# When the mixing stage's results are gated, and in which order the last rows leave

## The chip, the core and the metric

The kernel runs on one core of a Trainium2 chip. The metric is the device time of one execution in microseconds (us); the figure compared is the median of several runs. The engines are TensorE (PE, matmuls and transposes), VectorE (DVE), ScalarE (ACT), GpSimd (POOL) and SyncE (SP, which here only issues DMAs). Each engine works through its own queue in order.

## The reference

One decoder layer over 2048 rows of width 1024, in float32:

```python
u = x * (1 + scale) + shift                  # scale, shift, gate from SiLU(c) @ W_ada
q, k, v, a_gate, p_in, p_gate, m_a, m_p = split(u @ W_in)
a = (sliding_window_attention_with_sinks(q, k, v) * silu(a_gate)) @ W_attn_proj
p = (group_linear(causal_pool(p_in)) * pool_scale * silu(p_gate)) @ W_pool_proj
y = (sigmoid(m_a) * a + sigmoid(m_p) * p) @ W_out * (1 + gate)
x = layer_norm(alpha * x + y) * ln_gain + ln_bias
```

## The kernel before

Every large matrix product is done by blocks: a *quad* multiplies two row blocks of weights with a resident activation of two column halves, and gets its four 128 x 512 results by seven block products instead of eight (a Strassen-Winograd scheme, named B11, T1, T2, B21, T3, B22, T4 after the operand that the activation side holds). One operand set per name lies in SBUF (`sets`, shown by the profile as set_B or set_T). Float32 accuracy comes from splitting each operand into a rounded high part (cast on ACT) and a low part (a subtraction on DVE), and taking three of the four cross terms. So one product is 3 x 4 = 12 matmuls of 128 x 128 by 128 x 512.

Weights of a quad are split in pairs by `pair_split` (first, second and third pair), into four rotating tiles called w_set; T4's single block is split by `half_split`. High parts of these show up at lines 303 and 310, low parts at line 132 (`low`). Weights come by DMA as W and A; GpSimd prepares their sums (`sum1`, `mid`, `late`, lines 266 to 275).

Quads are worked on in groups of two. `back` finishes a group: for each quad T2 and B21, then T3 of the first quad, B22 of the first, T3 and B22 of the second, then both T4. `front` opens the next group: B11 and T1 of each of its quads. `ring` runs the groups of one phase. Each product is followed by `tick()`, which counts the steps (14 per group), runs the hooks written down for that position, and then whatever `defer(n, f)` put n ticks ahead. At the hooks stand the loads and splits of the next phase's operand sets (`set_steps`, with SPLIT_AT and FETCH_AT giving positions; those under 14 fall into the last group of a phase, the others into the first group of the next).

The results of a quad leave in the order B21's (first row block, first half), then after T3 (second block, second half, in the SBUF tile p5, summed at line 387), after B22 (first block, second half), and after T4 (second block, first half). `consume` takes each.

After attention come six phases in one block of code: a last gate group, then for each half s of the sequence an attention mix phase (`attn_quad`, two groups) and a pool mix phase (`pool_quad`, two groups), and an output phase (`out_quad`, four groups). In the mix phases `gates_ahead` loads the gates (ma or mp) from DRAM, half of them at the group's start and half two ticks later, and runs a sigmoid over each; `consume` multiplies each result by its gate (line 620, or 629), the pool quads also add it to the attention part (631) and store y.

In the output phase a result is added to alpha times x (line 709). Rows are normalised once both halves are there, rows 14 and 15 by `last_stats` and `last_norm` (680 to 696); the very last group is done one quad after the other by `finish_pairs`.

In the attention stages PE's work on scores and values is interleaved with quads that fill the gaps (`filling`). `take_p` sums the pool windows on GpSimd, then `second` scales and subtracts on DVE and multiplies on GpSimd. The attention loop starts each iteration on DVE with a reciprocal of the softmax sums; `closing` holds additions that are to follow it.

A scheduler sets the final order of each engine's queue: it goes by the order in which instructions were written down, and lets a later one go first where the earlier isn't ready by its own clock. Calls by `dve`, `act`, `pool`, `sp` are pinned behind the instruction that was written down just before them on that engine; calls by `nc.vector`, `nc.scalar` and so on are not.

Of the kernel before, what the change touches and what calls it, by code (L numbers as in the profile page):

```python
# [60 lines left out]
def kernel(  # L61
# [276 lines left out]
    def back(ph, grp, opened, nxt, own, tick):  # L338
# [5 lines left out]
        for q, (a, b, c, w, *copy) in zip(grp, opened):  # L344
# [19 lines left out]
            if len(copy) < 2:  # L364
                nc.vector.tensor_tensor(b, c, p5, ALU.add)
# [17 lines left out]
        def with_t3(x):  # L383
            q, b, c, p5 = st[x]
            product(c, w[x][1], "T3")
            tick()
            nc.vector.tensor_tensor(p5, c, p5, ALU.add)
# [20 lines left out]
        for q, b, c, p5 in st:  # L408
            product(c, lasts.pop(0) if lasts else half_split(ph, q.a22), "T4")
            tick()  # L410
            q.consume(ph, 1, 0, c)

    def finish_pairs(ph, grp, opened, tick):
# [18 lines left out]
        for x, q in enumerate(grp):  # L432
# [15 lines left out]
            tick()  # L448
            q.consume(ph, 0, 1, b)
            product(c, lasts[x], "T4")  # L450
# [56 lines left out]
    SPLIT_AT = (2, 3, 4, 5, 6, 7, 11, 12, 13, 14, 15, 16, 17, 18)  # L507
# [93 lines left out]
    def gates_ahead(name, s, m, raw):  # L601
        g = {}

        def ahead(ph, turn):
            for mi, t in (((0, 0), (1, 1)), ((0, 1), (1, 0)))[turn]:
                x = g[mi, t] = ph.c("g")
                sp.dma_start(x, gates_d[name][s, m + mi, t])
                if raw:
                    defer(1, lambda x=x: nc.scalar.activation(x, x, AF.Sigmoid))  # L609

        return g, ahead

    def attn_quad(s, m):
        g, ahead = gates_ahead("ma", s, m, True)

        def consume(ph, mi, t, src):
# [3 lines left out]
            nc.vector.tensor_tensor(ta[k][:, t * CH : (t + 1) * CH], src, g.pop((mi, t)), ALU.mult)  # L620

        return Quad((wap[m], wap[m + 1]), consume, ahead)

    def pool_quad(s, m):
        gates, ahead = gates_ahead("mp", s, m, True)

        def consume(ph, mi, t, src):
            g = gates.pop((mi, t))
            nc.vector.tensor_tensor(g, src, g, ALU.mult)
            dst = ta[m + mi][:, t * CH : (t + 1) * CH]  # L630
            nc.vector.tensor_tensor(dst, g, dst, ALU.add)
# [46 lines left out]

    def last_stats(row, n, zn):
        nc.vector.bn_stats(carry[:, row - 12, 6 * n : 6 * n + 6], zn)  # L680

    def last_norm(row, z):

        st, mv, rs = (carry[:, row - 12, a:b] for a, b in ((0, 12), (12, 14), (14, 15)))
        nc.vector.bn_aggr(mv, st)
        nc.vector.tensor_scalar(rs, mv[:, 1:2], EPS, None, ALU.add)
        nc.gpsimd.tensor_tensor(rs, rs, mhalf, ALU.pow)
        nc.vector.scalar_tensor_tensor(z, z, mv[:, 0:1], vec["gain"], ALU.subtract, ALU.mult)
        ending.append((row, z, rs))
        if row + 1 < S // P:  # L690
            return
        for row, z, rs in ending[::-1]:
            for n, q in enumerate((nc.sync, nc.scalar)):
                zn = cols(z, n)
                nc.vector.scalar_tensor_tensor(zn, zn, rs, cols(vec["lnb"], n), ALU.mult, ALU.add)
                q.dma_start(out[row * P : (row + 1) * P, n * CH : (n + 1) * CH], zn)

    ending = []
# [4 lines left out]
    def out_quad(k):  # L703
        def consume(ph, mi, n, src):
            row = k + mi
            z, n_done = zs[row]
            zs[row][1] += 1
            zn = cols(z, n)
            nc.vector.scalar_tensor_tensor(zn, zn, ALPHA, src, ALU.mult, ALU.add)
# [66 lines left out]
    def attention(ph, s, fills, post, opened):  # L776
# [56 lines left out]
        def take_p(m, t, acc):  # L833
# [841 lines left out]
```

## Time and profile before

| | us |
|---|---|
| median of 3 runs (1681.26 to 1681.58) | 1681.29 |
| the profiled execution | 1681.68 |
| its span, first to last instruction | 1679.9 |
| PE busy | 1642.9 |
| DVE busy | 1208.6 |
| ACT busy | 1026.3 |
| POOL busy | 949.3 |

A row of the timeline gives start, duration, engine, line of the code, operation, the tiles written and read, and in brackets how long the engine was idle before it and what ended that. Names are the tiles' names without numbers: mm, lg, pt and pv are accumulators in PSUM, w_set split weights, set_B and set_T operand sets, g a gate, wide a 128 x 1024 tile of rows, p the tile p5. A row with x12 joins that many instructions. A row of the busy time by stretch gives the stretch, its length, then busy time and count of PE, PEld (weight loads), DVE, ACT and POOL, the granted share of PE's clock, and the DMA share and rate.

### The profile page before, as it was taken

What the parts mean: (1) busy time and instruction counts of PE and PEld (TensorE: products, weight loads), DVE (VectorE), ACT (ScalarE), POOL (GpSimd) and SP (SyncE); (2) the same over time, 40 slices, a digit from 0 to 9 for tenths busy, and PEclk for the clock granted to TensorE, in tenths of its full rate; (3) what the DMA queues carried; (4) which work ended last, traced back from release to release, by engine and by line L of the source; (5) the groups of instructions that cost most, each with busy time, mean ns of one, the idle gap of its engine ahead of it and who ended that gap; (6) DMA issues with size and microseconds to landing.
All of it is one profiled execution on the core that took longest, in us unless ns stands there. A gap on an engine that the chain in (4) does not pass through costs nothing.

```text
span 1679.9 us, 24661 instructions
## 1 busy us (share of the span) xinstructions
PE 1642.9 (98%) x8058; PEld 1382.7 (82%) x8058; DVE 1208.6 (72%) x2156; ACT 1026.3 (61%) x2146; POOL 949.3 (57%) x710
## 2 busy tenths in 40 slices
PE   7999999999999999999999999999999999999997
PEld 6788888888888788888888888888878878878886
DVE  6955656676867867566467677777769896979777
ACT  4754547778778755334577777776647464554452
POOL 3343437585867838773376858597445453423442
PEclk9999999999999999999999999999999999999999
DMA  9688844343543578872432335345968896677443
GB/s 362 209 291 296 204 158 124 99 126 107 176 137 113 188 278 298 312 273 94 154 128 88 126 131 171 118 127 188 330 215 313 274 321 219 227 271 235 155 147 113
DMA packets 185971, 331.56 MB, mean 197 GB/s; under 512 B 18017, under 2 KB 43761, under 8 KB 185841
## 3 DMA queue, kind: packets, MB, share of 16 engines
q1 hardware_dynamic: 182720, 325.72, 56.8%
q10 hardware_dynamic: 3088, 4.23, 1.1%
q8 instruction: 64, 1.05, 0.3%
q14 instruction: 67, 0.54, 0.1%
q0 software_dynamic: 32, 0.02, 0.0%
HBM read 223.77 MB, written 109.28 MB: 198 GB/s over the span
## 4 chain that ended last, share of the span: by engine, by line
PE 80%; DVE 7%; DMA 5%; ACT 3%; issue 2%; POOL 2%; SPq 1%; POOLq 0%; DVEq 0%; ACTq 0%
PE mm L57 51%; PE lg L57 22%; PE pv L57 4%; PE pt L57 4%; DMA head_T<-in_wada_dram 1%; DMA g<-mp_d 1%; DVE w_set L132 1%; DVE L L57 1%; SPq L57 1%; DVE set_T L57 1%; DMA head_B<-in_wada_dram 1%; DVE room L57 1%; DVE w_set L57 0%; DMA g<-ma_d 0%; ACT g L609 0%
## 5 line engine op out<-in xcount | busy, mean ns | idle before, releaser
L57 PE MATMUL mm<-set_B,w_set 128*128 128x512 f32 x2664 | 652.6, 392 | 0.9 <-DVE w_set L57 0.4
L57 PEld LDWEIGHTS mm<-set_B,w_set 128*128 128x128 f32 x2664 | 495.8, 188 | 103.2 <-DVE w_set L57 0.8
L57 PE MATMUL mm<-set_T,w_set 128*128 128x512 f32 x1824 | 453.4, 395 | 2.1 <-DVE mm L57 1.2
L57 PE MATMUL lg<-set_T,w_set 128*128 128x512 f32 x1704 | 411.3, 391 | 7.6 <-ACT w_set L303 2.8
L57 PEld LDWEIGHTS mm<-set_T,w_set 128*128 128x128 f32 x1824 | 336.3, 188 | 70.8 <-DVE mm L57 4.2
L57 PEld LDWEIGHTS lg<-set_T,w_set 128*128 128x128 f32 x1704 | 319.6, 188 | 78.0 <-issue 3.7
L132 DVE TENSOR_TENSOR w_set<-W,w_set 128x1024 fp32r<-128x1024 f32 x137 | 192.5, 1405 | 142.3 <-ACT w_set L303 133.0
L303 ACT CAST w_set<-W 128x1024 fp32r<-128x1024 f32 x137 | 144.0, 1051 | 192.8 <-PE mm L57 148.3
L266 POOL TENSOR_TENSOR W<-W,A 128x512 f32<-128x512 f32 x46 | 73.5, 1598 | 271.6 <-DMA A<-in_win_dram 66.5
L57 POOL TENSOR_TENSOR w_set<-W,w_set 128x512 fp32r<-128x512 f32 x120 | 159.1, 1333 | 110.4 <-ACT w_set L57 108.6
L57 DVE TENSOR_TENSOR o<-pv,o 64x128 f32<-64x128 f32 x256 | 71.9, 281 | 96.8 <-ACT o L57 93.4
L57 POOL TENSOR_TENSOR W<-W 128x512 f32<-128x512 f32 x82 | 111.1, 1368 | 52.8 <-DVE sm L57 25.8
L57 ACT ACTIVATE L<-L,nm 128x257 f32<-128x257 f32 (+1 forms) x256 | 127.1, 498 | 17.8 <-DVE nm L57 8.2
L275 POOL TENSOR_TENSOR W<-W 128x512 f32<-128x512 f32 x46 | 71.9, 1563 | 103.9 <-DVE w_set L132 94.0
L270 POOL TENSOR_TENSOR W<-W 128x512 f32<-128x512 f32 x44 | 80.3, 1828 | 83.1 <-DVE w_set L132 66.7
L57 DVE CUSTOM_DVE_ANT_0 L<-lg,bt,nsink 128x256 f32<-128x256 f32 (+1 forms) x256 | 111.6, 473 | 15.2 <-DMA pg<-pg_d 10.8
L57 ACT CAST w_set<-W 128x512 fp32r<-128x512 f32 (+1 forms) x165 | 101.4, 628 | 24.4 <-POOL W L57 14.5
L57 ACT COPY o<-pv 64x256 f32<-64x256 f32 x128 | 47.3, 369 | 71.3 <-PE pv L57 70.1
L271 POOL TENSOR_TENSOR W<-W 128x512 f32<-128x512 f32 x44 | 69.1, 1570 | 32.4 <-DMA W<-in_win_dram 16.4
L57 ACT ACTIVATE L<-L,sm 128x256 f32<-128x256 f32 (+1 forms) x128 | 64.3, 502 | 36.6 <-DVE sm L57 36.2
L57 DVE TENSOR_TENSOR ptl<-pt,pth 128x512 fp32r<-128x512 f32 (+1 forms) x128 | 85.7, 669 | 1.0 <-ACT pth L57 0.9
L57 POOL TENSOR_TENSOR spare<-spare 128x512 f32<-128x512 f32 x48 | 80.2, 1679 | 8.1 <-ACT spare L57 6.0
(233 smaller groups left out, 2411.6 us busy)
## 6 DMA issues: line engine op xcount, KB each, us to landing
W<-in_win_dram SPq DMA_DIRECT2D x42, 512.0 KB, 5.8
W<-in_win_dram SPq DMA_DIRECT2D x42, 256.0 KB, 4.0
A<-in_win_dram SPq DMA_DIRECT2D x42, 256.0 KB, 4.9
ag_d<-sig SPq DMA_DIRECT2D x32, 256.0 KB, 5.9
pg_d<-sig SPq DMA_DIRECT2D x32, 256.0 KB, 4.4
pg<-pg_d SPq DMA_DIRECT2D x32, 256.0 KB, 3.2
pin_B<-fin SPq DMA_DIRECT2D x32, 256.0 KB, 2.0
ag<-ag_d SPq DMA_DIRECT2D x32, 256.0 KB, 3.1
```

The lines of the kernel that those rows point to most:

```text
L57: return lambda *args, **kw: self.tc.keep_in_program_order(op(*args, **kw))
L132: engine.tensor_tensor(dst, src, as32(hi), ALU.subtract)
L266: e.tensor_tensor(self.w[:, 1, :], self.w[:, 2, :], self.a22, ALU.add)
L270: e.tensor_tensor(x[:, 1, :], x[:, 1, :], x[:, 0, :], ALU.subtract)
L271: e.tensor_tensor(x[:, 2, :], x[:, 0, :], x[:, 2, :], ALU.subtract)
L275: e.tensor_tensor(x[:, 3, :], x[:, 3, :], x[:, 1, :], ALU.subtract)
L303: a.copy(by_two(hi), raw)
```

## The change

In the mix phases each result is gated two results later than before (`two_behind`): a result's use is kept until two more have come, the last two run one and two ticks after the group's last product. The multiplications and additions there are pinned (`dve`). The sigmoids are put off by 2, 3 or 4 ticks instead of 1. T4's blocks are split before the tick behind the first B22 instead of after it. The splits of set T2 move from positions 6 and 7 to 8 and 9. In the attention stages the pool scaling goes into `closing`, behind the next reciprocal. In the last quad B22 comes before T3, two results are added to their rows in two steps, T4 goes to an accumulator of its own, and the halves of row 14 leave before those of row 15, one of them before the last product's result.

```diff
@@ back
             if len(copy) < 2:
-                nc.vector.tensor_tensor(b, c, p5, ALU.add)
+                (dve if q.ahead else nc.vector).tensor_tensor(b, c, p5, ALU.add)
...
-            nc.vector.tensor_tensor(p5, c, p5, ALU.add)
+            (dve if q.ahead else nc.vector).tensor_tensor(p5, c, p5, ALU.add)
             q.consume(ph, 1, 1, p5)
-        def with_b22(x):
+        def with_b22(x, then=None):
             q, b, c, p5 = st[x]
             product(b, w[x][0], "B22")
+            if then:
+                then()
             tick()
...
             third(1)
-            with_b22(0)
-            lasts = [half_split(ph, q.a22) for q in grp]
+            with_b22(0, lambda: lasts.extend(half_split(ph, q.a22) for q in grp))
...
             q.consume(ph, 1, 0, c)
+        defer(1, lambda: use_up(1))
+        defer(2, use_up)
@@ finish_pairs, behind B21's consume
+            last = x + 1 == len(grp)
+            if last:
+                q.consume(ph, 1, 1, p5, True)
+                product(b, w3[0], "B22")
+                tick()
+                q.consume(ph, 0, 1, b)
             product(c, w3[1], "T3")
             tick()
-            nc.vector.tensor_tensor(p5, c, p5, ALU.add)
-            q.consume(ph, 1, 1, p5)
-            product(b, w3[0], "B22")
-            if x + 1 < len(grp):
+            if last:
+                q.consume(ph, 1, 1, c)
+                ending.pop(0)()
+                q.consume(ph, 1, 0, c, True)
+                c = a
+            else:
...
-            product(c, lasts[x], "T4")
+            product(c, lasts[x], "T4", last)
@@
-    SPLIT_AT = (2, 3, 4, 5, 6, 7, 11, 12, 13, 14, 15, 16, 17, 18)
+    SPLIT_AT = (2, 3, 4, 5, 8, 9, 11, 12, 13, 14, 15, 16, 17, 18)
@@ gates_ahead
-                    defer(1, lambda x=x: nc.scalar.activation(x, x, AF.Sigmoid))
+                    wait = {(0, 0): 2, (1, 1): 3, (0, 1): 2, (1, 0): 4}[mi, t]
+                    defer(wait, lambda x=x: nc.scalar.activation(x, x, AF.Sigmoid))
+    unused = []
+    def use_up(left=0):
+        while len(unused) > left:
+            unused.pop(0)()
+    def two_behind(use):
+        def consume(ph, mi, t, src):
+            use_up(1)
+            unused.append(lambda: use(ph, mi, t, src))
+        return consume
@@ attn_quad, pool_quad
-            nc.vector.tensor_tensor(ta[k][:, t * CH : (t + 1) * CH], src, g.pop((mi, t)), ALU.mult)
+            dve.tensor_tensor(ta[k][:, t * CH : (t + 1) * CH], src, g.pop((mi, t)), ALU.mult)
-        return Quad((wap[m], wap[m + 1]), consume, ahead)
+        return Quad((wap[m], wap[m + 1]), two_behind(consume), ahead)
-            nc.vector.tensor_tensor(g, src, g, ALU.mult)
+            dve.tensor_tensor(g, src, g, ALU.mult)
...
-            nc.vector.tensor_tensor(dst, g, dst, ALU.add)
-            defer(3, lambda: sp.dma_start(y_d[s, m + mi, t], dst))
-        return Quad((wpp[m], wpp[m + 1]), consume, ahead)
+            dve.tensor_tensor(dst, g, dst, ALU.add)
+            defer(1, lambda: sp.dma_start(y_d[s, m + mi, t], dst))
+        return Quad((wpp[m], wpp[m + 1]), two_behind(consume), ahead)
@@ rows 14 and 15
+    def last_halves(row, z, rs):
+        def half(n, q):
+            zn = cols(z, n)
+            dve.scalar_tensor_tensor(zn, zn, rs, cols(vec["lnb"], n), ALU.mult, ALU.add)
+            q.dma_start(out[row * P : (row + 1) * P, n * CH : (n + 1) * CH], zn)
+        return [lambda n=n, q=q: half(n, q) for n, q in enumerate((nc.sync, nc.scalar))]
...
-        ending.append((row, z, rs))
-        if row + 1 < S // P:
-            return
-        for row, z, rs in ending[::-1]:
-            for n, q in enumerate((nc.sync, nc.scalar)):
...
+        ending.extend(last_halves(row, z, rs))
+        if row + 1 == S // P:
+            for f in ending:
+                f()
@@ out_quad
+            e = dve if row > 13 else nc.vector
+            if (row, n) in begun:
+                e.tensor_tensor(zn, src, zn, ALU.add)
+            else:
+                e.scalar_tensor_tensor(zn, zn, ALPHA, src, ALU.mult, ALU.add)
+            if partly:
+                begun.add((row, n))
+                return
             zs[row][1] += 1
-            nc.vector.scalar_tensor_tensor(zn, zn, ALPHA, src, ALU.mult, ALU.add)
@@ take_p
             def second():
                 pg, p, copied = x
-                dve.scalar_tensor_tensor(
-                    p, p, 1.0 / POOL_W[m // 2], copied if own else acc, ALU.mult, ALU.subtract
-                )
-                pool.tensor_tensor(p, p, pg, ALU.mult)
+                def scaled():
+                    dve.scalar_tensor_tensor(
+                        p, p, 1.0 / POOL_W[m // 2], copied if own else acc, ALU.mult, ALU.subtract
+                    )
+                    pool.tensor_tensor(p, p, pg, ALU.mult)
+                closing.append(scaled)
                 later(n + wait + 1, lambda: keep_raw(pin_d[s], m, t, p))
@@ close, filling
             while closing:
-                x, name = closing.pop()
-                _, b, c, p5 = st[x]
-                dve.tensor_tensor(b if name == "T2" else p5, c, p5, ALU.add)
+                closing.pop(0)()
+        def add_up(x, name):
+            _, b, c, p5 = st[x]
+            dve.tensor_tensor(b if name == "T2" else p5, c, p5, ALU.add)
...
-                        closing.append((x, name))
+                        closing.insert(0, lambda x=x, name=name: add_up(x, name))
@@ behind the attention loop
         for _ in fill:
             pass
+        close()
         run_coming(True)
```

More of the change, by code (lines that the diff above doesn't have):

```diff
@@ L440, in finish_pairs @@
             q.consume(ph, 0, 0, a)
+            last = x + 1 == len(grp)
[4 more added lines that the diff above has]
+                q.consume(ph, 0, 1, b)
             product(c, w3[1], "T3")
             tick()
-            nc.vector.tensor_tensor(p5, c, p5, ALU.add)
-            q.consume(ph, 1, 1, p5)
-            product(b, w3[0], "B22")
-            if x + 1 < len(grp):
+            if last:
[4 more added lines that the diff above has]
+            else:
+                nc.vector.tensor_tensor(p5, c, p5, ALU.add)
+                q.consume(ph, 1, 1, p5)
+                product(b, w3[0], "B22")
                 got = begin(x + 1)
-            tick()
-            q.consume(ph, 0, 1, b)
-            product(c, lasts[x], "T4")
+                tick()
+                q.consume(ph, 0, 1, b)
+            product(c, lasts[x], "T4", last)
             tick()
@@ L703, in out_quad, with consume @@
     def out_quad(k):
-        def consume(ph, mi, n, src):
+        begun = set()
+        def consume(ph, mi, n, src, partly=False):
             row = k + mi
             z, n_done = zs[row]
+            zn = cols(z, n)
+            e = dve if row > 13 else nc.vector
[6 more added lines that the diff above has]
+                return
             zs[row][1] += 1
-            zn = cols(z, n)
-            nc.vector.scalar_tensor_tensor(zn, zn, ALPHA, src, ALU.mult, ALU.add)
             if row > 13:
```

13 lines of the change are left out of this document (5 added, 8 removed).

## The prediction

> **What bounds the kernel now.** I read the page first: its header, the busy line of TensorE (PE) and the chain that ended last. Then I read that chain in order of time, the timeline around every gap between PE's products, and busy time by stretch.
>
> ```profile
> span 1679.9 us, 24661 instructions
> PE 1642.9 (98%) x8058; PEld 1382.7 (82%) x8058; DVE 1208.6 (72%) x2156; ACT 1026.3 (61%) x2146; POOL 949.3 (57%) x710
> 1566.65 2.72 PE lg L57 x12
> ```
>
> PE is the bound: where it runs undisturbed, one product of 12 matmuls takes 2.72 us (0.227 per matmul, third line, from the chain in order of time). The change leaves the number of matmuls as it is, so it can win only what PE loses between products, and what follows the last one. Ends of matmuls are modelled, so I measure the losses from starts in the timeline. I went through the five phases that start at the mixing stage and found three losses of over 0.5 us in the stretch of 1200 to 1520 us, none of that size between there and the last product, and a tail of some 9 us. These rows carry the three losses, in order of time: the first attention mix group, the last pool group of half 0, the last pool group of half 1.
>
> ```profile
> 1217.88 1.28 ACT L609 ACT_TABLE_LOAD   x1 [2.30 <-DMA g<-ma_d]
> 1221.91 2.88 PE L57 MATMUL mm<-set_B,w_set 128*128 128x512 f32 x12
> 1222.22 2.19 ACT L609 ACTIVATE g<-g 128x512 f32<-128x512 f32 x4
> 1225.24 1.04 ACT L303 CAST w_set<-W 128x1024 fp32r<-128x1024 f32 x1
> 1226.34 3.01 PE L57 MATMUL lg<-set_T,w_set 128*128 128x512 f32 x12 [1.54 <-ACT w_set L303]
> ...
> 1351.93 1.98 PE L57 MATMUL lg<-set_T,w_set 128*128 128x512 f32 x8
> 1359.86 1.97 PE L57 MATMUL mm<-set_B,w_set 128*128 128x512 f32 x8
> 1362.19 1.19 PE L57 MATMUL mm<-set_B,w_set 128*128 128x512 f32 x4 [0.36 <-DVE w_set L132]
> ...
> 1496.51 2.88 PE L57 MATMUL lg<-set_T,w_set 128*128 128x512 f32 x12
> 1507.39 1.97 PE L57 MATMUL lg<-set_T,w_set 128*128 128x512 f32 x8
> 1507.79 3.47 DVE L132 TENSOR_TENSOR w_set<-A,w_set 128x512 fp32r<-128x512 f32 x2
> 1509.62 1.19 PE L57 MATMUL lg<-set_T,w_set 128*128 128x512 f32 x4 [0.25 <-DVE w_set L132]
> 1511.18 1.21 DVE L57 TENSOR_TENSOR set_T<-set_T 128x1024 fp32r<-128x1024 f32 x1
> 1512.31 0.68 DVE L387 TENSOR_TENSOR p<-lg,p 128x512 f32<-128x512 f32 x1
> 1513.14 4.53 PE L57 MATMUL lg<-set_T,w_set 128*128 128x512 f32 x12 [2.33 <-DVE p L387]
> 1517.51 2.68 PE L57 MATMUL mm<-set_B,w_set 128*128 128x512 f32 x11
> ```
>
> Loss A: B21 starts at 1221.91 and T3 at 1226.34, 4.43 instead of 2.72: 1.71 lost. Loss B: from the first T4 (1351.93) to the next B11 (1359.86) two products should take 5.44 and take 7.93: 2.49 lost; inside that B11 the last four matmuls start 2.33 after the first instead of 1.81: 0.52 more, 3.0 together. Loss C: the two T4 from 1507.39 to 1517.51 take 10.12: 4.68 lost. Of that the second T4 alone takes 4.53 instead of 2.72, about 1.8, because its matmuls run at half pace after an idle of 2.33. A, B and C make 9.4 us.
>
> The causes differ. At A it is ScalarE (ACT): the cast of T3's block (L303, 1225.24) stands behind eight sigmoids, the first of which waited 2.30 us for its gate's DMA. At B and C it is VectorE (DVE): T4's low half comes late by a little, and above all the second T4 may not write the accumulator before L387 has read it, and L387 stands in DVE's queue behind other work.
>
> ```profile
> 1319.20:1359.80 40.60, 38.69 (x170) 31.41 (x169) 32.46 (x33) 22.12 (x28) 18.93 (x12) 1.00 0.87 299
> 1474.70:1517.40 42.70, 40.12 (x169) 32.47 (x169) 31.63 (x33) 21.13 (x27) 10.69 (x7) 0.96 0.80 278
> 1493.28 4.02 ACT L609 ACTIVATE g<-g 128x512 f32<-128x512 f32 x6 [0.86 <-DMA g<-mp_d]
> 1502.01 2.35 DVE L57 TENSOR_TENSOR set_T<-set_T 128x1024 fp32r<-128x1024 f32 x1
> 1504.28 1.78 DVE L629 TENSOR_TENSOR g<-p,g 128x512 f32<-128x512 f32 x1
> 1505.99 0.68 DVE L629 TENSOR_TENSOR g<-mm,g 128x512 f32<-128x512 f32 x1
> 1506.59 1.28 DVE L631 TENSOR_TENSOR wide<-g,wide 128x512 f32<-128x512 f32 x2
> 1509.01 6.74 SPq L57 DMA_DIRECT2D y_d<-wide  x2
> ```
>
> The first two rows are stretches of the last pool groups (PE, PEld, DVE, ACT, POOL busy): DVE has 32.5 and 31.6 us to do in a group that PE alone would finish in 14 x 2.72 = 38.1. It is heavily loaded, not overloaded; so order decides, and a change of order can help or only move the queue.
>
> **The change part by part.** Gating two products later: no operation is added. In a pool group each of eight results costs one multiply and one add, 0.68 + 0.64. Results 1 and 2 now run after T3 and after the first B22 instead of after the first and second B21, 3 to 8 after two products more. What must be done on DVE before the second T4 then contains results 1 and 2 in the place of 3 and 4, so by itself it takes nothing out. What does take work out: the two casts of set T2 (SPLIT_AT) go from before to behind L387, one low part of 1.21 at least. T4's low parts (3.47 for both) now come before the set's part and the gating that stood in front of them. And result 3, which reads SBUF twice and took 1.78 instead of 0.68, goes behind L387.
>
> Worked out for C: T3 of the first quad starts at 1496.51 and ends at 1499.23. Behind that DVE has L387 0.68, result 1 1.32, T4's two low parts 3.47, a part of T1 2.35 at most (1.21 at least), result 2 1.32: 9.1 in all, done at 1508.4, plus some 0.5 of waiting for T4's first cast (an estimate: its buffer is held by that B22's high part, until 1499.23 + 1.81); then L387 ends at 1509.6. The second T4 is wanted at 1507.39 + 2.72 = 1510.11. The first T4's low half is wanted at 1509.2, and stands some 5 us ahead of that. That is 0.5 of slack on nine microseconds of queue, so I leave 0.4 of stall, and 4.3 of 4.68 is won, with the half pace that came of it. At B the same order holds: 2.7 of 3.0. Bounds for B and C together: 7.7 if all goes, 3 if half of the DVE queue only moves.
>
> Row and rule: the low parts, result 3 and the set's part took 1.7, 1.78 and 2.35 in this stretch against 0.68 for the same size reading PSUM once (1505.99). The Trainium skill, "SBUF — State Buffer", in its consequences of the port rules, says that a DVE instruction with two SBUF inputs and a GpSimd instruction that reads SBUF exclude each other, and that the one that comes second blocks. By that rule both adds of results 1 and 2 now fall where GpSimd prepares the next weights and each waits for it; that speaks against the change. By 1.78 against 0.68 this is 1.1 each, 4.4 in the two groups, and the sum for B and C would be 2.6 instead of 7.0 if all of it reached PE.
>
> Half pace: here an idle of 2.33 was enough for it (1513.14). The Trainium skill, "TensorE: Matmul & The Clock Gate", in Part 1, gives an idle window of about 3.4 us. By the row a new stall of over 2.3 costs some 1.8 on top, by the rule only one of over 3.4; the trace decides.
>
> Sigmoids spread: the same eight per group, two each at ticks 2, 3, 4 and 6 instead of four each at ticks 1 and 3. At A two of them (2 x 0.55, from the row of 1222.22) leave the path ahead of T3's cast: 1.1 of 1.71 won. The bounds are 0.6, if the table load waits for the same DMA and the cast waits elsewhere, and 1.71. At C the six that wait for the gate's DMA (1493.28) become four, so the set's cast behind them comes earlier; that is in C.
>
> Queues: the store of y is still issued at the same tick (use two later, store two ticks less behind the use), but SyncE's queue now reaches it nearer to DVE's add. It already stands 6.74 there for two stores. Behind it are the next group's weights and sets, which have 4 products or more of slack; I cost it at nothing, 0.5 if that cover is gone. Accumulators: the first quad's two banks come free at ticks 5 and 8, the second's at 6 and 10, the next front needs the first at tick 10 and the last at tick 13: nothing, as long as DVE is less than 2 products behind.
>
> Pool scaling behind a reciprocal: this is in the attention stages.
>
> ```profile
> 563.51 1.76 DVE L57 SCALAR_TENSOR_TENSOR fin<-fin,p 128x512 f32<-128x512 f32 x1 [2.32 <-POOL fin L57]
> 564.76 0.62 ACT L57 CAST w_set<-W 128x512 fp32r<-128x512 f32 x1 [4.30 <-POOL W L57]
> 565.20 0.15 DVE L57 RECIPROCAL sm<-sm 128x2 f32<-128x2 f32 x1
> 566.85 0.51 PE L57 MATMUL pv<-pth,vv 128*128 128x256 f32 x2 [1.40 <-ACT pth L57]
> ```
>
> It is the largest stall of the kind: the scaling waited 2.32 for GpSimd, took 1.76, and held the reciprocal. But ACT was itself held by GpSimd until 564.76, and DVE's low part for the value product still stands behind the scaling. So an earlier reciprocal brings nothing here: I take 0, between 1.4 won and 0.3 lost (32 scalings each 0.15 later, of which a bank might wait for two).
>
> Last rows in a new order: PE's five last products are the same, in another order.
>
> ```profile
> 1669.37 1.07 PE L57 MATMUL lg<-set_T,t4l 128*128 128x512 f32 x4
> 1670.71 0.68 DVE L709 SCALAR_TENSOR_TENSOR wide<-wide,lg 128x512 f32<-128x512 f32 x1
> 1671.31 0.74 DVE L695 SCALAR_TENSOR_TENSOR wide<-wide,carry,wide 128x512 f32<-128x512 f32 x1
> 1671.97 0.69 DVE L680 BATCH_NORM_STATS2 carry<-wide 128x6 f32<-128x512 f32 x1
> 1672.58 0.73 DVE L695 SCALAR_TENSOR_TENSOR wide<-wide,carry,wide 128x512 f32<-128x512 f32 x1
> 1673.23 0.20 DVE L685 BATCH_NORM_AGGREGATE carry<-carry 128x2 f32<-128x12 f32 x1
> 1673.54 1.28 DVE L688 SCALAR_TENSOR_TENSOR wide<-wide,carry,wide 128x1024 f32<-128x1024 f32 x1
> 1673.70 1.52 POOL L687 TENSOR_TENSOR carry<-carry,mhalf 128x1 f32<-128x1 f32 x1 [2.50 <-DVE carry L686]
> 1675.25 1.41 DVE L695 SCALAR_TENSOR_TENSOR wide<-wide,carry,wide 128x512 f32<-128x512 f32 x2 [0.44 <-POOL carry L687]
> ```
>
> Today the two halves of row 14 sit between the last sum, its statistics and the aggregate: two pitches of 0.65. Now one of them is done before the last T4 ends, and the other comes behind L688, where DVE waits 0.44 for GpSimd anyway; it costs 0.74 - 0.44 = 0.3 there. Before the last product ends DVE has one sum (0.68), statistics (0.69), that half (0.74) and a second partial sum (0.68), 2.8, against the product's 2.72: just hidden, 0.3 if not. The gain is 1.3 - 0.3 - up to 0.3: I take 0.7.
>
> Sum: 1.1 (A) + 7.0 (B, C) + 0.7 (end) = 8.8; I charge 0.5 for small new stalls, since the gated results now come, in the attention groups, ahead of the next front's low part. That makes 8.3 from the profiled execution's 1681.68 (its span 1679.9 and 1.8 around it), 1673.4; the median of the runs lies 0.4 lower, so 1673.0.
>
> **The rivals.** First, slower: the next front's low part becomes the late one. Everything that left the queue ahead of L387 now stands behind it: results 3 to 6 (4 x 1.32) and T2's two parts (2 x 1.21), all ahead of that low part (1.21) in program order. From L387's end at 1509.6 it would be done 8.9 later, at 1518.5, and at 1521.8 if three of these work beside GpSimd (1.78 instead of 0.68 each); the middle is 1520.1. B11, from 1510.11 + 2.72 on, wants it 1.81 after its start, at 1514.6. That is 5.5 of stall, and with 1.8 of half pace 7.3 in each of the two last pool groups, 14.6 instead of 7.7: 6.9 lost, less A and the end, 5.1 slower: 1686.4. For it: DVE's load above, and at B the low part already came 0.52 late. Against it: a multiply and the add that needs it can't follow at once, and in the rows of before other ready work stands between them (1504.28, 1505.99 and then the two adds), so the low part should slip in after result 3 or 4. It decides where the low part starts later than 1513.4 at C.
>
> Second, no change: DVE's queue is only moved and the same time is lost at other products; A and the end alone are won: 1679.5. It is also what comes if the scheduler floats the sigmoids back to their old places.
>
> Third, more: all of A, B, C and the end vanish and the attention's stalls behind the scaling too: 1681.3 - 9.4 - 1.0 - 1.4 = 1669.5. Against it stands ACT's row of 564.76.
>
> **How the numbers follow.** The forecast, 1673.0 (from 1671 to 1677 within its own bounds), gets 0.66; the low part late 0.14, between 1678 and 1690 by its bounds; no change 0.12; more 0.08. A measurement of this kernel can tell about 0.2%, 3.4 us, from no change: faster is below 1677.9, slower above 1684.7. Faster: 0.66 + 0.08 + 0.01 of the first rival's low end = 0.75. Same: 0.10 of no change and 0.05 of the first rival, 0.15. Slower: 0.08 of the first rival and 0.02 for a queue that I don't see, 0.10. The range runs from 1669.5 to 1681.0: it takes in the forecast, no change and the first rival's lower part, and leaves out its rest and half of "more", under 0.2.
>
> **What would show it.** Right: T3 of the first attention group starts within 1 us of B21's end; no product between 1330 and 1520 starts over 0.7 late; L387 ends before the second T4 is due; the sigmoids no longer follow a wait for the gates' DMA; the last statistics follow the last sum at once. Wrong: a wait of PE on the low part inside the B11 behind a pool group, matmuls at 0.43 us after it, or PE waiting for a bank that a gating still reads.

## The result, and the profile after

| times in us | before | after |
|---|---|---|
| median of the runs (16 each) | 1680.72 | 1684.36 |
| lowest to highest | 1679.51 to 1682.11 | 1681.94 to 1687.21 |
| profiled execution, and its span | 1681.68, 1679.9 | 1683.62, 1681.8 |

The changed kernel is slower: the ratio is 1.0024, 95% interval 1.0017 to 1.0031, some 2.9 to 5.2 us. The forecast was 8.3 us faster.

The page of after, header and busy line of PE: the same matmuls, the same busy time but for 0.4 us.

```profile
span 1681.8 us, 24678 instructions
PE 1643.3 (98%) x8058; PEld 1383.0 (82%) x8058; DVE 1204.1 (72%) x2157; ACT 1024.7 (61%) x2146; POOL 948.9 (56%) x710
```

The timeline of after, at the places of losses A, B and C, in order of time.

```profile
1221.32 2.88 PE L57 MATMUL mm<-set_B,w_set 128*128 128x512 f32 x12
1224.04 2.88 PE L57 MATMUL lg<-set_T,w_set 128*128 128x512 f32 x12
...
1354.63 5.60 PE L57 MATMUL lg<-set_T,w_set 128*128 128x512 f32 x24
1360.07 2.88 PE L57 MATMUL mm<-set_B,w_set 128*128 128x512 f32 x12
1365.51 1.98 PE L57 MATMUL mm<-set_B,w_set 128*128 128x512 f32 x8
1369.72 1.20 PE L57 MATMUL mm<-set_B,w_set 128*128 128x512 f32 x4 [2.24 <-DVE w_set L132]
...
1509.49 5.60 PE L57 MATMUL lg<-set_T,w_set 128*128 128x512 f32 x24
1514.93 2.88 PE L57 MATMUL mm<-set_B,w_set 128*128 128x512 f32 x12
1520.37 1.98 PE L57 MATMUL mm<-set_B,w_set 128*128 128x512 f32 x8
1525.04 1.21 PE L57 MATMUL mm<-set_B,w_set 128*128 128x512 f32 x4 [2.70 <-DVE w_set L132]
1526.09 4.50 PE L57 MATMUL mm<-set_T,w_set 128*128 128x512 f32 x12
```

Loss A is gone: T3 (1224.04) starts 2.72 behind B21. Both T4 of a group now run without a gap (the x24 rows), and so does the first quad's B11. But each of the last pool groups has a new stall one quad further on: the *second* quad's B11 waits 2.24 and 2.70 for the low part of its own weights (L132), and at C the next product then runs at a slower pace (4.50 for 12 matmuls instead of 2.88).

The other change is in the attention stages. The wait rows name engine and tile, what was waited for, then total us, times and longest; they cover 262 to 605 us, first PE and ACT of after, then ACT of before.

```profile
PE mm L57 <- ACT mm L57: 2.3, 2, 1.2
ACT raw L57 <- DMA ma_d<-raw: 6.4, 3, 3.1
```

```profile
ACT raw L57 <- DMA ma_d<-raw: 0.2, 1, 0.2
```

ACT's copies into the tile raw now wait 6.4 us for the DMA that stores the copy before (`take_gate` has one buffer of it), and PE waits for ACT's copy of an accumulator, which it did not before. One such place in the timeline, of after:

```profile
450.68 1.10 POOL L57 TENSOR_TENSOR nxt<-vb 128x518 f32<-128x518 f32 x1
454.30 1.30 POOL L57 TENSOR_TENSOR fin<-fin,pg 128x512 f32<-128x512 f32 x1
455.63 0.32 SPq L57 DMA_DIRECT2D pin_B<-fin  x1
457.63 0.55 SPq L57 DMA_DIRECT2D ma_d<-raw  x1
463.90 0.59 ACT L57 COPY raw<-mm 128x512 f32<-128x512 f32 x1 [3.10 <-DMA ma_d<-raw]
464.38 0.59 ACT L57 COPY mm<-mm 128x512 f32<-128x512 f32 x1
465.03 1.20 PE L57 MATMUL mm<-set_T,w_set 128*128 128x512 f32 x4 [1.24 <-ACT mm L57]
```

and of before:

```profile
450.88 1.34 POOL L57 TENSOR_TENSOR fin<-fin,pg 128x512 f32<-128x512 f32 x1
452.19 1.50 POOL L57 TENSOR_TENSOR nxt<-vb 128x518 f32<-128x518 f32 x1
452.25 0.32 SPq L57 DMA_DIRECT2D pin_B<-fin  x1
461.03 0.56 ACT L57 COPY raw<-mm 128x512 f32<-128x512 f32 x1
```

Since the scaling sits behind the next reciprocal, the multiply that follows it on GpSimd (fin<-fin,pg) now stands behind the next result's window sums (nxt), 3.4 us later. SyncE (SPq) stands at the store of that result until then, and the store of raw stands behind it in the same queue; ACT's next raw copy, its copy of the accumulator and PE's product follow.

To put numbers on stretches I sum, over all matmuls, the time from one start to the next above the median of that shape (us lost). A profile is one execution, so the medians beside them count for more.

| kernel | attention, 400 to 1165 | mix, 1200 to 1530 |
|---|---|---|
| before | 14.3 | 9.6 |
| after | 19.7 | 6.7 |

So in the two traces the attention stages lost 5.4 us, and the mix phases won 2.9 where 8.1 had been forecast for them.

### The profile page after: what moved, and what is told of

It is laid out like the page before. It is cut to its first block, busy times and chain, and to the rows that moved or that the text cites. A ratio compares the mean times of both kernels' runs of the same rounds, so it can differ in the third digit from the quotient of the medians.

```text
span 1681.8 us, 24678 instructions
## 1 busy us (share of the span) xinstructions
PE 1643.3 (98%) x8058; PEld 1383.0 (82%) x8058; DVE 1204.1 (72%) x2157; ACT 1024.7 (61%) x2146; POOL 948.9 (56%) x710
## 4 chain that ended last, share of the span: by engine, by line
PE 78%; DVE 7%; POOL 5%; ACT 4%; DMA 4%; issue 3%; SPq 0%; DVEq 0%; POOLq 0%; ACTq 0%
PE mm L57 48%; PE lg L57 23%; PE pv L57 4%; PE pt L57 3%; DMA ma_d<-raw 1%; POOL nxt L57 1%; DVE wide L57 1%; POOL W L57 1%; ACT L L57 1%; ACT w_set L57 1%; POOL fin L57 1%; DVE w_set L57 1%; POOL w_set L57 1%; DVE w_set L132 1%; DVE set_T L57 1%
## 5 line engine op out<-in xcount | busy, mean ns | idle before, releaser
L132 DVE TENSOR_TENSOR w_set<-W,w_set 128x1024 fp32r<-128x1024 f32 x137 | 194.7, 1421 | 144.4 <-ACT w_set L303 135.7
L57 POOL TENSOR_TENSOR spare<-spare 128x512 f32<-128x512 f32 x48 | 83.6, 1749 | 11.6 <-ACT spare L57 7.0
```

Source lines behind the costliest of these rows:

```text
L57: return lambda *args, **kw: self.tc.keep_in_program_order(op(*args, **kw))
L132: engine.tensor_tensor(dst, src, as32(hi), ALU.subtract)
```

## The experiments

Times are medians; each ratio is to runs of the kernel before on the same chip, with its 95% interval.

**The parts one by one.** First the changed kernel with the attention part taken back:

```diff
-                closing.append(scaled)     # scaling and multiply behind the next reciprocal
+                scaled()                   # at once, as before
```

> The changed kernel with the attention stages as before (the pool scaling in its old place, the additions put behind the reciprocal as before); the mix phases and the last rows changed. Theory (the attention stages lose 5 us because the scaling's multiply now comes behind the next window sums on GpSimd, and the stores and copies behind it are late): 4 to 5.5 us faster than the changed kernel, so 1678 to 1680.5, that is 1 to 3 faster than before. Rival 1 (the mix phases are the loss, low parts late there): about 1684, as the changed kernel. Rival 2 (the three parts only add up to a different fall of the DMAs, and none is the cause): within 1.5 of before.

Measured 1680.56, ratio 0.9998 (0.9989 to 1.0006). The loss against the kernel before is gone, but the 1 to 3 us below it that the theory had forecast didn't come, and by its time alone the second rival fits as well. The same edit the other way round, the attention part alone on the kernel before:

> The kernel before with nothing but the pool scaling behind the next reciprocal. Theory: 4 to 5.5 us slower than before, 1685 to 1686, and the trace shows PE waiting for ACT's copy of an accumulator at the same products as in the changed kernel (5 waits of 0.7 to 1.6 us). Rival 1: within 1 us of before. What I predicted: 0, between 1.4 faster and 0.3 slower.

Measured 1684.39, ratio 1.0023 (1.0014 to 1.0032): 4.1 us slower, by itself all that the whole change costs. PE's waits on ACT's accumulator copy are there (464.50, 571.58, 1039.30, 1147.11; together 3.2 us), in the trace of a kernel with nothing else changed. The last rows alone:

> The kernel before with nothing but the last quad and the last rows in the new order. By the trace of the changed kernel (from the last product's start to the end 9.99 us against 9.81): 0 to 0.3 slower than before. By the prediction: 0.7 faster. Rival: the pinned order holds something in the last groups up and it is 1 or more slower.

Measured 1680.11, ratio 0.9998 (0.9989 to 1.0006), an interval that holds nothing as well as the 0.7 won that had been forecast. And the mix phases alone:

> The kernel before with nothing but the mix phases changed (gated two results later, sigmoids spread, T4's blocks cast first, the splits of set T2 later). Theory: 2 to 3 us faster than before, 1678 to 1679.5: the losses of 9.4 us in those phases become about 7 because the second quad's first low part is now late behind the last pool groups. Rival 1 (the mix phases as the loss): 3 us or more slower. The prediction's sum for this part was 7.6 faster, 1673.

Measured 1680.93, ratio 1.0004 (0.9995 to 1.0012). My theory missed here, as the prediction had: no gain at all. Its profile has 6.3 us lost in the mix phases, but that execution (1678.08) was among its fastest. In the profile of the first experiment, with the same mix phases, they cost 11.0: the stalls were longer (2.42 and 3.37, against 1.76 and 2.69), and both were followed by matmuls at half pace. The second of them:

```profile
1523.63 2.08 PE L57 MATMUL mm<-set_B,w_set 128*128 128x512 f32 x4 [3.37 <-DVE w_set L132]
1525.51 4.80 PE L57 MATMUL mm<-set_T,w_set 128*128 128x512 f32 x12
```

**The attention part: which link.** Two edits of the changed kernel. In the first, the store waits one iteration longer, so that SyncE need not stand at it:

```diff
-                later(n + wait + 1, lambda: keep_raw(pin_d[s], m, t, p))
+                later(n + wait + 2, lambda: keep_raw(pin_d[s], m, t, p))
```

> The changed kernel with the store of a pool result (pin_B<-fin) issued one iteration of the attention loop later, nothing else. Theory (SyncE stands at that store until GpSimd's multiply, which is late; the gate store ma_d<-raw and the weight loads behind it wait, so ACT's next copy into the single tile raw is late and PE waits for ACT's accumulator copy): SyncE no longer stands, most of the 4 us come back: 1680.5 to 1682 against 1684.4. Rival (GpSimd itself is late, through the weight sums and low parts it prepares behind the multiply, and the store only shows it): within 1 us of the changed kernel. Second rival: the tile fin is held longer and GpSimd waits for it instead: 1685 or more.

Measured 1683.16, ratio 1.0017 (1.0008 to 1.0025). In 262 to 605 us the wait on ma_d<-raw is gone and PE's waits on the accumulator copy too, so the SyncE link is real. But about 1 us came back, not 3, and its interval overlaps that of the changed kernel (1.0017 to 1.0031). PE now waits in another place:

```profile
566.20 0.62 ACT L57 CAST w_set<-W 128x512 fp32r<-128x512 f32 x1 [4.76 <-POOL W L57]
568.28 0.50 PE L57 MATMUL pv<-pth,vv 128*128 128x256 f32 x2 [2.13 <-ACT pth L57]
```

ACT's cast stands for GpSimd's weight sums (before: 4.30 at the same cast, and 1.40 for PE), and over both attention stages PE's waits for ACT's cast of pth come to 4.9, against 2.4 before and 1.3 in the changed kernel. That fits the rival for the rest: GpSimd is late there, and the store was one way in which that reached PE. It isn't shown, for pace is in it too: the mean granted clock of these runs was 0.9949, that of the runs of before beside them 0.9969, by estimate 3.4 us of 1680. The second edit keeps the late scaling, but puts each result's window sums at least two iterations behind the last one's:

```diff
-            n = max(now_n[0], pool_free[1] + 1, pool_free[0] + 3)
+            n = max(now_n[0], pool_free[1] + 2, pool_free[0] + 3)
```

> The changed kernel with the next pool result's window sums at least two iterations behind the last one's, so that the multiply that is put off stands ahead of them again on GpSimd. Theory (it is the multiply standing behind the window sums that makes store, raw and copy late): 3 to 4 us come back, about 1681. Rival (it is the scaling's place on DVE, behind the reciprocal, that costs): within 1 us of the changed kernel, 1684. Second rival: the accumulators are held one iteration longer and PE waits for a bank: 1685 or more.

Measured 1678.89, ratio 0.9997 (0.9988 to 1.0006): the whole 4 us are back, and the loss in the attention stages falls from 19.7 to 14.6. But this doesn't show that the order of multiply and window sums is the cause, since the edit didn't restore the order. In the trace 6 of the 32 multiplies still start behind window sums that began after their scaling had ended, as many as in the changed kernel (before: 2). One of them, with the wait of PE that comes of it:

```profile
556.87 0.67 DVE L57 SCALAR_TENSOR_TENSOR fin<-fin,mm 128x512 f32<-128x512 f32 x1
558.66 1.06 POOL L57 TENSOR_TENSOR nxt<-vb 128x526 f32<-128x526 f32 x1
563.87 1.34 POOL L57 TENSOR_TENSOR fin<-fin,pg 128x512 f32<-128x512 f32 x1
569.25 1.43 PE L57 MATMUL mm<-set_T,w_set 128*128 128x512 f32 x5 [1.72 <-ACT mm L57]
```

The chain through raw is there too. ACT's wait for the store of raw, in 262 to 605 us, is as long as in the changed kernel (6.4), and over both stages PE's waits for ACT's copy of an accumulator come to 4.3 in either trace.

```profile
ACT raw L57 <- DMA ma_d<-raw: 6.3, 2, 3.9
```

So the later window sums won the 4 us elsewhere; where isn't shown. The last two kernels below bear it out: without the late scaling the same edit wins about as much.

**The mix phases: delay or pinning.** Next, the mix part alone with each result gated one later instead of two:

```diff
-        defer(1, lambda: use_up(1))
-        defer(2, use_up)
+        defer(1, use_up)
...
-            use_up(1)
+            use_up()
             unused.append(lambda: use(ph, mi, t, src))
...
-            defer(1, lambda: sp.dma_start(y_d[s, m + mi, t], dst))
+            defer(2, lambda: sp.dma_start(y_d[s, m + mi, t], dst))
```

> The mix phases alone as changed, on the kernel before, but each result gated one result later instead of two. Theory for the mix phases (DVE has no idle time left between the second T3 of the last pool group and the next front, gating two behind moves some 2.6 us of work into it, and the second quad's low part comes last): about half of that is back, the stall inside the second B11 behind each last pool group falls from 1.9 and 2.9 us to under 1.5, and the time is 1 to 2 us less than with two behind, 1679 to 1680. Rival (SyncE's stand at the y stores delays the set's fetch and with it the low part): the stall stays, 1680.9.

Measured 1681.40, ratio 1.0008 (0.9999 to 1.0017): a miss. The stalls in the second B11 were 2.9 and 2.3, not under 1.5, so within the intervals a delay by one result costs as much as one by two. The rival had forecast just that; what speaks against it is the next kernel, where SyncE stands at the stores of y as well (at C 3.94 and 3.89) and PE doesn't stall there. Then the kernel before with only the sigmoids spread, T4's casts first and set T2 later, and no delay:

```diff
...
-            with_b22(0)
-            lasts = [half_split(ph, q.a22) for q in grp]
+            with_b22(0, lambda: lasts.extend(half_split(ph, q.a22) for q in grp))
...
-    SPLIT_AT = (2, 3, 4, 5, 6, 7, 11, 12, 13, 14, 15, 16, 17, 18)
+    SPLIT_AT = (2, 3, 4, 5, 8, 9, 11, 12, 13, 14, 15, 16, 17, 18)
...
-                    defer(1, lambda x=x: nc.scalar.activation(x, x, AF.Sigmoid))
+                    wait = {(0, 0): 2, (1, 1): 3, (0, 1): 2, (1, 0): 4}[mi, t]
+                    defer(wait, lambda x=x: nc.scalar.activation(x, x, AF.Sigmoid))
```

> The kernel before with the sigmoids spread, T4's blocks cast before the tick, and the splits of set T2 two positions later; each result is gated at once as before, multiplications and additions not pinned. Theory: loss A (1.7 us) goes, and T4's low parts are on time; of losses B and C at most a half stays, so 2 to 4 us faster than before, 1676.5 to 1678.5. Rival (without the gating put off, the sum that frees the accumulator stays late): A alone, 1.7 faster, 1678.5 to 1679. Second rival (whatever leaves the queue ahead of that sum comes back at the next low part): no gain, 1680.

Measured 1676.22, ratio 0.9977 (0.9968 to 0.9986): 4 us faster than before. The mix phases lose 2.7 us in its profile, and C is gone; what is left is at B, 0.59 ahead of the second T4 and 1.62 in the second quad's B11. It differs from the whole mix part in two things, the delay and the pinning. So one kernel is the whole mix part with the pinning and no delay:

```diff
...
-        return Quad((wpp[m], wpp[m + 1]), two_behind(consume), ahead)
+        return Quad((wpp[m], wpp[m + 1]), consume, ahead)
...
```

> The mix phases as changed on the kernel before, but every result gated at once; the pinning of the multiplications and additions stays. It differs from the kernel that was 4.0 us faster only in the pinning, and from the whole mix part only in the delay. Theory (the delay of the gating costs what the rest of the mix part wins): 3 to 5 us faster than before, 1675.5 to 1677.5. Rival (the pinning, which keeps a low part from slipping between a multiply and its add, costs it): within 1.5 us of before, 1679 to 1682.

Measured 1676.85, ratio 0.9978 (0.9970 to 0.9987). Another has the delay and no pinning, here and at the other multiplications and additions:

```diff
...
-            dve.tensor_tensor(g, src, g, ALU.mult)
+            nc.vector.tensor_tensor(g, src, g, ALU.mult)
...
```

> The mix phases as changed on the kernel before, gated two results later, but none of the multiplications and additions pinned. Theory (the delay costs): as the pinned one, 1680 to 1682. Rival (the pinning costs): 3 us or more faster than before, under 1677.5.

Measured 1677.56, ratio 0.9976 (0.9967 to 0.9985). Both are fast: my theory holds for the first and fell for the second, and so did its rival, for which the first should have been slow. So only delay and pin together are slow. The rows of DVE tell why. They show the sum of the first T3 (p<-lg,p) in the last pool group and the multiply that gates it (g<-p,g): the whole mix part, gated at once, and delayed but not pinned.

```profile
1496.06 0.69 DVE L57 TENSOR_TENSOR p<-lg,p 128x512 f32<-128x512 f32 x1 [0.49 <-PE lg L57]
1504.45 1.19 DVE L57 TENSOR_TENSOR g<-p,g 128x512 f32<-128x512 f32 x1
```

```profile
1497.81 0.68 DVE L387 TENSOR_TENSOR p<-lg,p 128x512 f32<-128x512 f32 x1
1498.52 0.69 DVE L631 TENSOR_TENSOR g<-p,g 128x512 f32<-128x512 f32 x1
```

```profile
1499.13 0.68 DVE L387 TENSOR_TENSOR p<-lg,p 128x512 f32<-128x512 f32 x1
1499.85 0.69 DVE L647 TENSOR_TENSOR g<-p,g 128x512 f32<-128x512 f32 x1
```

Without the pin the scheduler moves this late-written multiply back to 0.7 us behind its sum, as if it had not been delayed; with the pin it comes 8.4 us behind. So a delay that is carried out costs, and the pin carries it out. At C, what it costs is idle time. Busy time by stretch, the 15 us ahead of the first T4 of the last pool group (DVE is the third engine), in the same three kernels:

```profile
1489.02:1504.02 15.00, 15.00 (x67) 12.39 (x67) 12.05 (x14) 11.31 (x17) 3.61 (x3) 1.00 1.03 345
```

```profile
1490.36:1505.36 15.00, 15.00 (x67) 12.40 (x67) 14.23 (x17) 11.29 (x17) 3.61 (x3) 1.00 1.07 362
```

```profile
1491.78:1506.78 15.00, 15.00 (x67) 12.40 (x67) 14.32 (x17) 11.30 (x17) 3.38 (x3) 1.00 1.09 366
```

Delayed, DVE is 2.2 us less busy before the T4; in the 15 us after it, it is busy for 14.9 to 15.0 in all three. What it left undone comes out at the last thing due in that stretch, the second quad's low part:

```profile
1518.31 1.21 DVE L132 TENSOR_TENSOR w_set<-W,w_set 128x1024 fp32r<-128x1024 f32 x1
1519.57 2.07 PE L57 MATMUL mm<-set_B,w_set 128*128 128x512 f32 x4 [2.69 <-DVE w_set L132]
```

```profile
1516.24 2.88 PE L57 MATMUL mm<-set_B,w_set 128*128 128x512 f32 x12
1516.54 1.21 DVE L132 TENSOR_TENSOR w_set<-W,w_set 128x1024 fp32r<-128x1024 f32 x1
```

In the whole mix part (first fence) it ends 4.6 us after its product's start at 1514.90, gated at once (second fence) 1.5 after. That is 3.1 for 2.2 of idle; the rest is the order within the queue, where one part of set B (1516.57, 1.21) stands ahead of it in the first kernel and behind it (1518.27) in the second.

The other kernels agree at C. Pinned but gated at once, DVE is busy for 13.64 of the 15 us, and the second quad's B11 waits 0.24; gated one result later it is 13.07 and 2.10. At B the idle doesn't explain the stall: there the kernel that gates at once is busy for 14.93 and waits 1.62, the whole mix part for 13.15 and 1.76, the one gated one later for 14.19 and 2.71. So the account by idle time is shown for C alone.

**What is worth keeping.** The mix part that gates at once, with the late scaling and the later window sums (the edit of pool_free above):

> The kernel before with the sigmoids spread, T4's blocks cast first and set T2 split later, each result gated at once, plus the pool scaling behind the reciprocal with the next window sums two iterations behind. If the two parts add up (4.0 faster, and 1 to 2 faster for the second, from the changed kernel's two variants): 1674 to 1676. If the order of the sums only takes back what the late scaling costs: 1676 to 1677.

Measured 1675.89, ratio 0.9971 (0.9959 to 0.9982). And the same without the late scaling (`scaled()` at once, as in the first diff):

> The same without the late scaling: scaling and multiply in their old place, only the next window sums two iterations behind the last one's. If the scaling behind the reciprocal is worth nothing by itself (as predicted): within 1 us of the one with it. If it is worth its 1.4 us once the multiply stands ahead of the sums: 1 to 2 us slower than the one with it.

Measured 1673.14, ratio 0.9955 (0.9943 to 0.9968): 7.4 us faster than before, and the best of all. I had expected it to be no better than the one with the late scaling; it is 2.8 us better, and the runs, 5 and 6 of them, don't overlap (1672.50 to 1674.37 against 1674.52 to 1676.41). So the late scaling costs something with the later sums too. With it, 6 of the 32 multiplies again stand behind window sums, and ACT waits for the store of raw in 262 to 605 us (first row); without it, none does, and ACT hardly waits (second row).

```profile
ACT raw L57 <- DMA ma_d<-raw: 6.3, 2, 3.9
```

```profile
ACT raw L57 <- DMA ma_d<-raw: 0.2, 1, 0.2
```

The later window sums are what is new in this kernel against the one that only gates at once (0.9977): by themselves they win some 3.7 us, on two chips, each against the kernel before on its own. That is close to what they won in the changed kernel, and the late scaling costs 4.1 without them and 2.8 with them.

## Why the prediction was wrong

**Pool scaling: the step that failed most.** It was priced at 0, "between 1.4 won and 0.3 lost", and cost 4.1. The price looked at DVE (the idle of 2.32, the reciprocal) and at ACT. But a scaling that is moved takes its multiply along, and that one changes its place in GpSimd's queue, and the store behind it in SyncE's. I counted the 32 scalings on DVE and not the queues of the two engines that they feed. The cost is shown by the attention part alone, and the chain through the store of raw by the traces: it is there in every kernel profiled with the late scaling, but for the one whose store waits longer, and in none without it (0.2 us at most). How the cost divides stays open: without the chain some 3 us were left, and no kernel had the late scaling with every multiply ahead of the next sums.

**Gating two later: the right mechanism, followed to the wrong product.** Right were: L387 ahead of the second T4, T4's low parts on time, and the first low part slipping in between two results (after: L132 at 1513.33, between a multiply and its add). The step that failed is "it takes nothing out" by itself, and what does take work out leaves 0.4 of stall. It counted what stands ahead of the second T4, with DVE busy without a break. It didn't count that a result put off leaves DVE idle at the time when it could have been gated (at C 12.05 us busy of the 15 ahead of the first T4, against 14.23 gated at once), nor did it go on to the second quad's low part, for which PE waits 2.24 and 2.70. The first rival had the mechanism, and "decides where the low part starts later than 1513.4": the first started at 1513.33, the second is the one that came late. Of the 7.0 for B and C nothing was left in the median of the mix part alone (0.7 slower, interval 0.8 faster to 2.0 slower). Without the delay the three edits that I held for helpers won 4.0.

**Row and rule.** The Trainium skill, "SBUF — State Buffer", in its consequences of the port rules, has a DVE instruction with two SBUF inputs contend with a GpSimd instruction that reads SBUF. The prediction weighed that with 1.1 for each of the adds of results 1 and 2, 4.4 in all. These took no longer than beside nothing (first row), and result 3, as before, was the one to wait (second row). The price was not paid at the place that I gave it: GpSimd began its weight sums at 1503.35 and 1509.05, just as these adds (1502.85 and 1508.71) ended. In the rows that the price came from, the set's part is twice the size of the others; its 2.35 stands against 1.21, not 0.68.

```profile
1508.71 0.69 DVE L57 TENSOR_TENSOR wide<-g,wide 128x512 f32<-128x512 f32 x1
1511.14 1.66 DVE L57 TENSOR_TENSOR wide<-g,wide 128x512 f32<-128x512 f32 x1
```

**Loss C was too dear by 1.8.** The half pace behind its stall was in the profile shown, and I took it as part of the loss in every execution. The kernel with only the last rows changed runs the same code there, with the same idle:

```profile
1512.01 2.98 PE L57 MATMUL lg<-set_T,w_set 128*128 128x512 f32 x12 [2.33 <-DVE p L387]
```

2.98 instead of 4.53 behind an idle of 2.33 in both. C is 2.9 in one execution and 4.7 in another. The half pace itself makes 1.55 of that; the 1.8 of the prediction set the length of a row, 4.53, against a pitch of 2.72.

**Sigmoids: right, and more.** 1.1 was taken of A; T3 starts on time, 1.7 won.

**Last rows: 0.7 taken, about 0.15 found**, in one trace each. From the start of the last four matmuls to the end of the span it is 10.53 before (1669.37 to 1679.9) and 10.38 after (1671.42 to 1681.8). Last rows of DVE in after:

```profile
1669.58 1.28 DVE L57 SCALAR_TENSOR_TENSOR wide<-wide,carry,wide 128x1024 f32<-128x1024 f32 x1
1670.77 0.68 DVE L57 TENSOR_TENSOR wide<-lg,wide 128x512 f32<-128x512 f32 x1
1672.10 0.74 DVE L57 SCALAR_TENSOR_TENSOR wide<-wide,carry,wide 128x512 f32<-128x512 f32 x1
1672.75 0.68 DVE L57 SCALAR_TENSOR_TENSOR wide<-wide,lg 128x512 f32<-128x512 f32 x1
1673.54 0.69 DVE L57 TENSOR_TENSOR wide<-mm,wide 128x512 f32<-128x512 f32 x1
1675.31 3.26 DVE L57 SCALAR_TENSOR_TENSOR wide<-wide,carry,wide 128x1024 f32<-128x1024 f32 x4
```

"2.8 against the product's 2.72, just hidden" left out the first row: row 14's own scaling of 1.28 stands ahead of T3's sum, so the four steps start 1.0 behind that product's end (1666.89 + 2.88), and the last sum (1673.54) comes 2.12 behind the start of the last matmuls instead of 1.34. Most of what the new order wins at the end is lost there.

**Queues: "nothing", not settled.** SyncE's longest row at the stores of y is no longer than before (4.36 against 6.74), but ACT's cast of the next set waits longer for its fetch: 6.24 at B (1364.89) and 5.92 at C, against 0.23 and 3.02 before. PE never waited for that set in the trace, and the kernel that gates at once has SyncE standing 3.9 twice without a stall of PE there. I didn't try it alone.

**The sum.** Forecast 8.3 faster, measured 3.6 slower. By runs of each part alone attention costs 4.1 instead of 0, and the mix phases cost 0.7 where 8.1 was to be won; at the end 0.5 of the 0.7 is missing. Together the parts make 1 us more than the whole, which their intervals allow. The chances were wrong with it: the time lies outside the range, 1684.36 is still "same" (0.15) by the prediction's own bounds, and by the interval it is slower, which got 0.10. Two mechanisms led there, one of which wasn't among the rivals but for the 0.02 of "a queue that I don't see".

## What to carry to other kernels

Follow a moved instruction to everything that its result feeds: here the price lay one and two queues further on, in a multiply that came late on GpSimd, and in part in a store that held back another store in the same queue whose tile had one buffer. An edit that wins time back has not shown the cause until it is tried on the kernel without the fault, and the order that it was to restore is looked up in the trace. An engine that saturates later is better not left idle earlier, so use a result as soon as it is there and move only what nobody waits for; and after a wait is freed, price the next two deadlines of that engine, not one. A delay written into the program is only a delay if the scheduler is bound to it, so read in the trace where the instruction ended up before giving it the credit or the blame.

## What was not expected of the hardware

Whether half pace follows a stall differed from execution to execution. Behind an idle of 2.33 (before) 12 matmuls took 4.53, and behind the same 2.33 in another kernel 2.98; behind 2.24 in after (1369.72) nothing slowed down, behind 2.70 it began only some 1.5 us later, and in the kernel gated one later an idle of 2.10 was enough (1522.54). The slow phases behind these stalls lasted some 3 to 6 us and cost 1.4 to 2.8. The Trainium skill, "TensorE: Matmul & The Clock Gate", in Part 1, describes a free-running window of about 3.4 us, which fits both the chance and the length; that an idle of 2.1 to 2.7, less than a window, is sometimes enough is what these traces add. It shows in the medians too: the mean granted clock of the mix part's runs was 0.9957, of 35 runs of before beside them 0.9969. 0.0012 of 1680 is 2.0 us, so by this estimate a part of what the mix phases won in waits went back as pace. The three kernels that don't carry out the delay had 0.9975 to 0.9978: of the 4.5 us between the first of them and the whole mix part, 3 would be pace by the same estimate, and the rest the stalls themselves.
